# Stores to scratch on GpSimd's queue, and contraction halves of even and odd tiles, in an encoder layer

## The chip, the core and the metric

The kernel runs on one core of a Trainium2 chip. The metric is the device time of one execution in microseconds, as the median of several runs. The profile is of one execution. In it, PE is the tensor engine, ACT the scalar engine, DVE the vector engine, POOL is GpSimd, and SP is the engine that does nothing here but issue transfers. Each has a program of its own that it works through in order; an instruction that has to wait holds back all that follow it on its engine.

## What is computed

One layer of a bidirectional encoder in float32, for 1024 positions of width 2048. Cut to what matters:

```
mod = silu(c) @ w_ada + b_ada                    # 2048 x 6144
shift, scale, gate = split(mod, 3)
h = rmsnorm(x, pre_g) * (1 + scale) + shift
q, k, v, gate_a, u, gate_p = split(h @ w_in)     # 2048 x 4608
y_a = windowed_gqa(q, k, v, rel_table, sink) * silu(gate_a)
y_p = multiscale_pool(u, w_pool_grp, pool_scale) * silu(gate_p)
g_a, g_p = split(sigmoid(h @ w_merge + b_merge)) # 2048 x 4096
merged = g_a * (y_a @ w_br_attn) + g_p * (y_p @ w_br_pool)   # 1024 x 2048 each
out = x + gate * rmsnorm(merged @ w_out, post_g) # 2048 x 2048
```

## The kernel before

**Matrix products.** A float32 product is made of three float32r products: `split` writes a rounded copy `hi` on ACT and the rest `lo` on DVE, and PE forms hi·hi, lo·hi and hi·lo. On top of that the large products use Strassen's scheme in Winograd's form: `strassen` takes a weight block of 256 columns (a pair) and two halves of the contraction, and forms seven products in place of eight. The moving sides (B11, T3, T2, B21, T4, T1, B22) are made once from h and stay in SBUF; the weight sides are made anew for each pair, from the four blocks a11, a12, a21, a22 of 128 x 128 tiles that `load_raws` fetches (tag "raw", four buffers, so that a pair is fetched ahead). The products accumulate in the PSUM banks X, V and Z. A pair of four tiles a half is 84 matmuls.

**Passes.** The contraction over 2048 does not fit into SBUF at once. `PART` cuts its 16 tiles of 128 into two passes: `pass1` computes the first part for all 34 pairs of `w_in` and `w_merge` and stores it to `part_d` (four stores of 256 KB a pair, `to_dram`, L283); the second pass, `next_pair`, loads these sums (`load_parts`, L189), adds its own and stores to `proj_d`. In a pass the halves of the contraction are tiles j and j + 8. The first four pairs of the first pass run in two rounds of two tiles a half (`ramp_pair`, the ramp, with `ramp_d`), so that products can begin before all of h is there.

**The head.** Before the first pair x is loaded and normed (`fetch_rows_of_x`, `norm_rows`) and half of it turned. For each j the modulation columns of tiles j and j + 8, scale and shift, come from 16 loads of `w_ada` (`ada_slots`, L407, and `ada_tile`, L388; 4 segments of 128 columns a row) and products with c on PE (`modulation`, L421). `fill(j)` then modulates the tiles and writes the moving sides; for j = 0 and 2 GpSimd takes three subtractions (L98), for j = 1 and 3 two.

**Other work beside the pairs.** Small steps hang in a list `side` that `run` serves between products: the modulation of j = 4 to 7, the gate's row (`gate_step`, `gate_row`), the bias lines, turning the rest of x, then attention (`step`, with `ya_d`) and pooling (`window`, `mix`, with `yp_d`; two memsets of u in each window run on GpSimd). Then come the two branches (L961; `finish` multiplies by a gate from `proj_d`, stores the first branch to `mp_d` and adds it in the second, with two buffers "pv", and stores to `m_d`), the first half of the output product by Strassen (`out_pair`, `po_d`), and the rest of it with the norm and the output (`finish_rows`).

**Buffers of a pair's results.** They have the tag "ev": nine buffers at the start of the first pass, six at its end, seven in the second pass. A pair needs four for the loaded sums and three for p7, u2 and u4 (L262, `u4`, copies Z on ACT). A buffer is free once the store from it has landed.

**Order.** All transfers but seven small ones are issued by SP: `load` and `store` are both `nc.sync.dma_start`. A planner orders each engine's instructions by a model of their times, so loads and stores come mixed in SP's program.

Of the kernel before, what the change touches and what calls it, by code (L numbers as in the profile page):

```python
# [42 lines left out]
def encoder_layer(ctx: ExitStack, tc: tile.TileContext, x, c, table, w_ada, b_ada, pre_g,  # L43
# [56 lines left out]
    load = nc.sync.dma_start  # L100
    store = nc.sync.dma_start

# [8 lines left out]
    sc = const.tile([P, KT], F32, name="sc")  # L111
    modc = const.tile([P, 4, HALF], F32, name="modc")
    rstd = const.tile([P, NB], F32, name="rstd")
# [57 lines left out]

    def load_raws(w, n0, krow, js):
        raws = []
        nj = len(js)
        joint = wp.tile([P, 2, 2, nj, P], F32, tag="raw", name=uid("raw"), bufs=4) if nj < 4 else None
        for nt in range(2):
            r = joint[:, nt] if nj < 4 else wp.tile([P, 2, nj, P], F32, tag="raw", name=uid("raw"), bufs=4)
            for kh in range(2):
                r0 = krow(kh, js[0])
                load(r[:, kh], w[r0:r0 + nj * P, n0 + nt * P:n0 + (nt + 1) * P]  # L180
                     .rearrange("(k p) n -> p k n", p=P))
            raws.append(r)
        return raws

    def load_parts(ev, part):
# [5 lines left out]

    def strassen(w, n0, krow, js, op, ev, finish, part=None, raws=None):

# [6 lines left out]

        nj = len(js)
        raws = raws or load_raws(w, n0, krow, js)
        a11, a12, a21, a22 = raws[0][:, 0], raws[0][:, 1], raws[1][:, 0], raws[1][:, 1]
        parts = load_parts(ev, part) if callable(part) else part
# [104 lines left out]

    def krow1(part):  # L310
        return lambda kh, j: (kh * HALF + part * 4 + j) * P


# [25 lines left out]

    PART = [[0, 1, 2, 3, 8, 9, 10, 11], [4, 5, 6, 7, 12, 13, 14, 15]]  # L340
    xT = {}
    for s in range(2):
        for k in PART[0]:
            if k % 8 == 3:
# [12 lines left out]
    def norm_rows(si):  # L357
# [13 lines left out]
        for q in range(2):  # L371
            xt = xts[si, 2 * q]
            nc.vector.tensor_scalar(xt, xt, rstd[:, si:si + 1], None, op0=ALU.mult)
            pt = bank(("mm", SEEDED[si % 2])[q], "XT1")
            for j in range(4):
                nc.tensor.transpose(pt[:, j * P:(j + 1) * P], xt[:, j * P:(j + 1) * P], ident)
            for j in range(4):
                dst = xT[q * 8 + j, si // 4][:, (si % 4) * P:(si % 4 + 1) * P]
                if j % 2 == 0:
                    nc.vector.tensor_copy(dst, pt[:, j * P:(j + 1) * P])  # L380
                else:
                    nc.scalar.activation(dst, pt[:, j * P:(j + 1) * P], AF.Copy)

    def ada_tile(j, q):
        at = xa.tile([P, 2, 4, P], F32, tag="xa", name=uid("ada"))
        for kk in range(2):
            r0 = (2 * q + kk) * P
            load(at[:, kk], w_ada[r0:r0 + P, 0:2 * D].rearrange("p (g n) -> p g n", g=4)  # L388
                 [:, :, j * P:(j + 1) * P])
        return at  # L390
# [7 lines left out]
    def mod_columns(j, pm):  # L398
        add(modc[:, :, j], pm[:, 0:4], cols[:, 16 + j:16 + j + 25:8])
        nc.vector.scalar_tensor_tensor(modc[:, 2:4, j], modc[:, 2:4, j], 1.0,  # L400
                                       cols[:, 48 + j:48 + j + 9:8], op0=ALU.add, op1=ALU.mult)

    def ada_slots(j):
        tiles = []
        for kc in range(KT):
            tiles.append(slot("ada", F32, (P, 4, P)))
            load(tiles[kc], w_ada[kc * P:(kc + 1) * P, 0:2 * D].rearrange("p (g n) -> p g n", g=4)  # L407
                 [:, :, j * P:(j + 1) * P])
        return tiles
# [49 lines left out]
    def modulate(eng, t, k):  # L459
        kh, j = k // HALF, k % HALF  # L460
        if eng is nc.scalar:
            eng.activation(t, t, AF.Identity, scale=modc[:, 2 + kh, j:j + 1], bias=modc[:, kh, j:j + 1])
        else:
            eng.tensor_scalar(t, t, modc[:, 2 + kh, j:j + 1], modc[:, kh, j:j + 1],
                              op0=ALU.mult, op1=ALU.add)
# [13 lines left out]
    def fill(j, eng):  # L479
        (b11, b12), (b21, b22) = ((xT[k, 0], xT[k, 1]) for k in (j, j + 8))  # L480
        modulate(nc.scalar, b11, j)
        modulate(nc.vector, b12, j)
        modulate(nc.vector, b22, j + 8)
        modulate(nc.scalar, b21, j + 8)
        put(op, "B11", j, b11)
# [13 lines left out]
    claim(0)  # L499
    raws = [load_raws(*weight_of(ORDER[i]), krow1(0), [0, 1]) for i in range(RAMP)]  # L500
    ada.append(ada_slots(2))
# [25 lines left out]
    def ramp_pair(jj, i, parts, at):  # L527
        w, n0 = weight_of(ORDER[i])
        dst = block(part_d, ORDER[i]) if jj else block(ramp_d[i], 0)
        run(strassen(w, n0, krow1(0), (2 * jj, 2 * jj + 1), op, ev, to_dram(dst), parts, raws[i]),  # L530
            side, range(7), at)
# [5 lines left out]
    raws = [load_raws(*weight_of(ORDER[i]), krow1(0), (2, 3)) for i in range(RAMP)]  # L537
    fill(2, nc.gpsimd)
# [10 lines left out]
    def pass1(n, side, every):  # L549
        nonlocal i  # L550
        for k in range(n):
            w, n0 = weight_of(ORDER[i])
            run(strassen(w, n0, krow1(0), range(4), op, ev, to_dram(block(part_d, ORDER[i]))),
                side, every[k % len(every)])
# [31 lines left out]
    def gate_row(n):  # L586
# [33 lines left out]
    def fetch_x(si, q):  # L620
        xt = xin.tile([P, 512], F32, tag="xt2", name=uid("xt"))
        c0 = q * 1024 + 512
        load(xt, x[si * P:(si + 1) * P, c0:c0 + 512])
# [3 lines left out]
    def turn_x(si, q, xt):  # L627
# [3 lines left out]
        for j in range(4):  # L631
            dst = h[q * 8 + 4 + j][si // 4][:, (si % 4) * P:(si % 4 + 1) * P]
            nc.scalar.activation(dst, pt[:, j * P:(j + 1) * P], AF.Copy)
# [10 lines left out]
    side.extend(lambda k=k, s=s: modulate((nc.scalar, nc.vector)[s], h[k][s], k) for k in PART[1] for s in range(2))  # L644
    h1, h2, t2 = {j: h[4 + j] for j in range(4)}, {j: h[12 + j] for j in range(4)}, {}

# [16 lines left out]
    def next_pair(every=(0, 1, 3, 4, 6)):  # L663
        n = ORDER[pidx[0]]
        w, n0 = weight_of(n)
        run(strassen(w, n0, krow1(1), range(4), op, ev, to_dram(block(proj_d, n)),
                     block(part_d, n)), side, every)
# [232 lines left out]
    for b, w in enumerate((w_ba, w_bp)):  # L900
# [36 lines left out]
        for i in range(8):  # L937
            def finish(blk, ps, addend, res, gates=gates, i=i, b=b):
# [21 lines left out]

            run(strassen(w, i * 256, lambda kh, j: (kh * 4 + j) * P, range(4), op, ev, finish), side,  # L961
                () if b == 0 and i == 0 else (0, 2, 4) if b == 0 or i < 7 else (0, 1, 2, 3))
# [176 lines left out]
    def finish_rows(o, ssq, half, t):  # L1139
# [6 lines left out]
        for n in (1, 0, 2, 3):  # L1146
# [91 lines left out]
```

## Time and profile before

| | us |
|---|---|
| median of 3 runs | 2189.49 (2187.74 to 2189.76) |
| profiled execution, time | 2183.51 |
| profiled execution, span of its instructions | 2181.6 |
| PE busy | 2131.1 (98%) |
| DVE busy | 1480.4 (68%) |
| ACT busy | 1071.4 (49%) |
| GpSimd busy | 90.9 (4%) |
| mean granted clock of PE | 0.993 |

In a row of the timeline the columns are the start, the time that it covers, engine, line, operation, output and inputs by the program's names, shapes, count, and in brackets the idle time before it and what ended it. "SPq" is the issue of a transfer. In a table by stage each engine has its busy time and, in brackets, the number of instructions; then come the granted clock, the share of the DMA engines that was busy (a value above 1 means that transfers overlap on them) and the rate. In a table of waits the columns are the sum, the count and the longest. PE's busy time is modelled for matmuls that overlap, so it can include short stalls.

### The profile page before, as it was taken

Reading aid. Unit: us, or ns where it says so; the run is one execution under the profiler, and the core shown is the slowest. Engines: PE = TensorE matmul, PEld = TensorE weight load, DVE = VectorE, ACT = ScalarE, POOL = GpSimd, SP = SyncE. Lnnn points to the kernel's source line nnn. Section 1 sums busy time; section 2 is a strip of 40 time slices with the busy share of each in tenths; the row PEclk is TensorE's granted clock in tenths of the full one; section 3 lists DMA queues with packets and bytes.
Section 4 is the critical chain, followed back from the end, with each engine's and each line's share of the span. In section 5 each row is a group of like instructions: output and inputs, shape, how many; then the busy total and the mean of one; then the engine's idle time right before and its main releaser. Section 6 shows DMA issues by size and latency. Waiting matters only on the chain.

```text
span 2181.6 us, 30031 instructions
## 1 busy us (share of the span) xinstructions
PE 2131.1 (98%) x10253; PEld 1761.0 (81%) x10253; DVE 1480.4 (68%) x2636; ACT 1071.4 (49%) x2024; POOL 90.9 (4%) x121
## 2 busy tenths in 40 slices
PE   5999999999999999999999999999999999999998
PEld 2488888888688888888888888888787888999886
DVE  6687665666445676777776887657858878755456
ACT  5464444444366546767765433334646545323353
POOL 1100000000000000000000000000000000000363
PEclk9999999999999999999999999999999999999999
DMA  9987666664444356555545666755755654539455
GB/s 299 267 254 214 193 189 192 199 217 151 134 152 126 116 175 202 164 169 173 167 154 192 218 224 204 245 171 180 224 162 162 203 175 149 189 97 309 138 199 184
DMA packets 403180, 410.58 MB, mean 188 GB/s; under 512 B 23723, under 2 KB 279851, under 8 KB 403028
## 3 DMA queue, kind: packets, MB, share of 16 engines
q1 hardware_dynamic: 402692, 408.62, 59.3%
q8 instruction: 80, 1.31, 0.3%
q14 instruction: 72, 0.59, 0.1%
q10 hardware_dynamic: 336, 0.06, 0.0%
HBM read 295.32 MB, written 115.37 MB: 188 GB/s over the span
## 4 chain that ended last, share of the span: by engine, by line
PE 92%; DMA 3%; DVE 3%; ACT 1%; issue 1%; SPq 0%; DVEq 0%; ACTq 0%
PE Z L216 30%; PE V L216 20%; PE X L216 20%; PE OUT L1115 3%; PE OUT L1114 3%; PE OUT L1113 3%; PE OUT L1028 2%; PE OUT L1029 2%; PE OUT L1027 2%; PE GEMV L421 2%; PE PT L757 1%; DMA raw<-in_w_in_dram 1%; DMA gt<-proj_d 1%; DMA xt<-in_x_dram 1%; PE PV L768 0%
## 5 line engine op out<-in xcount | busy, mean ns | idle before, releaser
L91 ACT ACTIVATE whi<-raw 128x512 fp32r<-128x512 f32 (+1 forms) x584 | 356.1, 612 | 615.2 <-PE Z L216 274.8
L92 DVE TENSOR_TENSOR wlo<-raw,whi 128x512 fp32r<-128x512 f32 (+1 forms) x584 | 400.6, 689 | 283.1 <-PE Z L216 170.3
L1028 PE MATMUL OUT<-wlo,mh 128*128 128x256 f32 x448 | 127.5, 285 | 3.1 <-DVE wlo L92 3.0
L1027 PE MATMUL OUT<-whi,mh 128*128 128x256 f32 x448 | 126.5, 284 | 1.2 <-DVE c L941 1.2
L1029 PE MATMUL OUT<-whi,ml 128*128 128x256 f32 x448 | 126.7, 284 | 0.0
L95 DVE TENSOR_TENSOR u<-V,u 128x512 f32<-128x512 f32 x88 | 60.6, 689 | 91.2 <-PE V L216 91.0
L216 PE MATMUL V<-T3h,whi 128*128 128x512 f32 x336 | 92.6, 394 | 4.4 <-ACT whi L91 4.4
L216 PE MATMUL Z<-B22h,whi 128*128 128x512 f32 x336 | 92.4, 394 | 1.0 <-ACT u L262 1.0
L216 PE MATMUL X<-B11h,whi 128*128 128x512 f32 x336 | 92.5, 393 | 0.5 <-ACT whi L91 0.5
L216 PE MATMUL Z<-T1h,whi 128*128 128x512 f32 x336 | 92.2, 392 | 0.5 <-ACT T1h L91 0.4
L216 PE MATMUL V<-T4h,whi 128*128 128x512 f32 x336 | 92.2, 392 | 0.0
L216 PE MATMUL X<-B11l,whi 128*128 128x512 f32 x336 | 91.2, 390 | 0.0
L216 PE MATMUL Z<-T2h,whi 128*128 128x512 f32 x336 | 91.2, 391 | 0.0
L216 PE MATMUL X<-B21h,whi 128*128 128x512 f32 x336 | 90.9, 390 | 0.0
L216 PE MATMUL Z<-B22l,whi 128*128 128x512 f32 x336 | 90.9, 390 | 0.0
L216 PE MATMUL Z<-T1l,whi 128*128 128x512 f32 x336 | 90.9, 389 | 0.0
L216 PE MATMUL V<-T4l,whi 128*128 128x512 f32 x336 | 90.9, 390 | 0.0
L216 PE MATMUL V<-T3h,wlo 128*128 128x512 f32 x336 | 90.9, 390 | 0.0
L216 PE MATMUL Z<-T2h,wlo 128*128 128x512 f32 x336 | 90.8, 390 | 0.0
L216 PE MATMUL V<-T4h,wlo 128*128 128x512 f32 x336 | 90.8, 390 | 0.0
L216 PE MATMUL Z<-B22h,wlo 128*128 128x512 f32 x336 | 90.8, 389 | 0.0
L216 PE MATMUL V<-T3l,whi 128*128 128x512 f32 x336 | 90.7, 390 | 0.0
(285 smaller groups left out, 4961.3 us busy)
## 6 DMA issues: line engine op xcount, KB each, us to landing
part<-part_d SPq DMA_DIRECT2D x136, 256.0 KB
ada<-in_w_ada_dram SPq DMA_DIRECT2D x128, 256.0 KB
raw<-in_w_in_dram SPq DMA_DIRECT2D x128, 256.0 KB
raw<-in_w_merge_dram SPq DMA_DIRECT2D x128, 256.0 KB
proj_d<-part SPq DMA_DIRECT2D x68, 256.0 KB
gada<-in_w_ada_dram SPq DMA_DIRECT2D x32, 512.0 KB
gt<-proj_d SPq DMA_DIRECT2D x64, 256.0 KB
raw<-in_w_out_dram SPq DMA_DIRECT2D x32, 512.0 KB
```

The source lines that it names most:

```text
L91: nc.scalar.activation(hi, src, AF.Copy)
L92: nc.vector.tensor_tensor(lo, src, f32(hi), ALU.subtract)
L95: (eng or nc.vector).tensor_tensor(o, a, b, ALU.add)
L216: nc.tensor.matmul(ps, w_[:, i], op[mov][j][m_], start=fresh and i == 0 and n == 0, stop=i == nj - 1 and n == 2, skip_group_check=True)
L421: nc.tensor.matmul(pv[g:g + 32, :], scz[:, kc, :], tile_of(kc), start=kc < 4, stop=kc >= 12, tile_position=(0, g))
L757: nc.tensor.transpose(pt[:, i * P:(i + 1) * P], p[:, i * P:(i + 1) * P], ident)
L1027: nc.tensor.matmul(o_, hi[:, ts_], wh, start=j == 0, stop=False)
L1028: nc.tensor.matmul(o_, hi[:, ts_], wl, start=False, stop=False)
L1029: nc.tensor.matmul(o_, lo[:, ts_], wh, start=False, stop=j == KS - 1)
L1113: nc.tensor.matmul(pb, hi[:, ts_], wh, start=k == KP[0], stop=False)
L1114: nc.tensor.matmul(pb, hi[:, ts_], wl, start=False, stop=False)
L1115: nc.tensor.matmul(pb, lo[:, ts_], wh, start=False, stop=k == KT - 1)
```

## The change

It has two parts. Stores to scratch, which all go through `store`, are issued by GpSimd; loads stay on SP, and so do the stores of the output. The two small loads of `gate_row` go to GpSimd too. And the halves of the contraction in the two passes become the even and the odd tiles: part 0 is tiles 0 to 7, and tile 2j stands in one half and 2j + 1 in the other. With that the columns of `w_ada` for one j are 2 segments of 256, x is turned by its first and then its second half, and `load_raws` fetches the 256 columns of a pair in one row of 1 KB (before: two of 512 bytes in loads of their own), two loads a pair in place of four. In the branches the halves stay as they were (`rows_apart`), but the rows are of 256 columns as well. The blocks a11 to a22 become strided slices of the raw tiles.

```diff
     load = nc.sync.dma_start
-    store = nc.sync.dma_start
+    store = nc.gpsimd.dma_start
...
-    def load_raws(w, n0, krow, js):
+    def load_raws(w, n0, rows, js):
         raws = []
         nj = len(js)
-        joint = wp.tile([P, 2, 2, nj, P], F32, tag="raw", ...) if nj < 4 else None
-        for nt in range(2):
-            r = joint[:, nt] if nj < 4 else wp.tile([P, 2, nj, P], F32, tag="raw", ...)
-            for kh in range(2):
-                r0 = krow(kh, js[0])
-                load(r[:, kh], w[r0:r0 + nj * P, n0 + nt * P:n0 + (nt + 1) * P]
-                     .rearrange("(k p) n -> p k n", p=P))
+        joint = wp.tile([P, 2, nj, 256], F32, tag="raw", ...) if nj < 4 else None
+        for kh in range(2):
+            r = joint[:, kh] if nj < 4 else wp.tile([P, nj, 256], F32, tag="raw", ...)
+            load(r, rows(w, js, kh)[:, :, n0:n0 + 256])
             raws.append(r)
         return raws
+
+    def rows_apart(w, js, kh):
+        r0 = (kh * len(js) + js[0]) * P
+        return w[r0:r0 + len(js) * P].rearrange("(k p) n -> p k n", p=P)
+
+    def rows_in_turn(part):
+        def rows(w, js, kh):
+            r0 = (part * 8 + 2 * js[0]) * P
+            return w[r0:r0 + 2 * len(js) * P].rearrange("(k h p) n -> h p k n", h=2, p=P)[kh]
+        return rows
...
-        a11, a12, a21, a22 = raws[0][:, 0], raws[0][:, 1], raws[1][:, 0], raws[1][:, 1]
+        a11, a21, a12, a22 = (raws[kh][:, :, nt * P:(nt + 1) * P] for kh in range(2) for nt in range(2))
...
-    PART = [[0, 1, 2, 3, 8, 9, 10, 11], [4, 5, 6, 7, 12, 13, 14, 15]]
+    PART = [range(8), range(8, 16)]
...
-            xt = xts[si, 2 * q]
+            xt = xts[si, q]
...
-            load(tiles[kc], w_ada[kc * P:(kc + 1) * P, 0:2 * D].rearrange("p (g n) -> p g n", g=4)
-                 [:, :, j * P:(j + 1) * P])
+            load(tiles[kc].rearrange("p (g h) n -> p g (h n)", g=2),
+                 w_ada[kc * P:(kc + 1) * P, 0:2 * D].rearrange("p (g n) -> p g n", g=2)
+                 [:, :, j * 256:(j + 1) * 256])
...
     def modulate(eng, t, k):
-        kh, j = k // HALF, k % HALF
+        j, kh = k // 2, k % 2
...
-        (b11, b12), (b21, b22) = ((xT[k, 0], xT[k, 1]) for k in (j, j + 8))
+        (b11, b12), (b21, b22) = ((xT[k, 0], xT[k, 1]) for k in (2 * j, 2 * j + 1))
...
-        load(grow[:, 0, :], b_ada[0:1, 2 * D + n * 256:2 * D + (n + 1) * 256])
-        load(grow[:, 1, :], post_g[0:1, sl])
+        nc.gpsimd.dma_start(grow[:, 0, :], b_ada[0:1, 2 * D + n * 256:2 * D + (n + 1) * 256])
+        nc.gpsimd.dma_start(grow[:, 1, :], post_g[0:1, sl])
...
-            store(out[r0:r0 + P, n * 512:(n + 1) * 512], o[t][n])
+            nc.sync.dma_start(out[r0:r0 + P, n * 512:(n + 1) * 512], o[t][n])
```

The remaining lines of the diff give the new tile numbers and the new shape of `modc` to the places that use them.

More of the change, by code (lines that the diff above doesn't have):

```diff
@@ L499, in encoder_layer @@
     claim(0)
-    raws = [load_raws(*weight_of(ORDER[i]), krow1(0), [0, 1]) for i in range(RAMP)]
+    raws = [load_raws(*weight_of(ORDER[i]), rows_in_turn(0), [0, 1]) for i in range(RAMP)]
     ada.append(ada_slots(2))
@@ L529, in ramp_pair @@
         dst = block(part_d, ORDER[i]) if jj else block(ramp_d[i], 0)
[L530 removed]
+        run(strassen(w, n0, rows_in_turn(0), (2 * jj, 2 * jj + 1), op, ev, to_dram(dst), parts, raws[i]),
             side, range(7), at)
@@ L536, in encoder_layer @@
                   if i == RAMP - 1 else None)
-    raws = [load_raws(*weight_of(ORDER[i]), krow1(0), (2, 3)) for i in range(RAMP)]
+    raws = [load_raws(*weight_of(ORDER[i]), rows_in_turn(0), (2, 3)) for i in range(RAMP)]
     fill(2, nc.gpsimd)
@@ L552, in pass1 @@
             w, n0 = weight_of(ORDER[i])
-            run(strassen(w, n0, krow1(0), range(4), op, ev, to_dram(block(part_d, ORDER[i]))),
+            run(strassen(w, n0, rows_in_turn(0), range(4), op, ev, to_dram(block(part_d, ORDER[i]))),
                 side, every[k % len(every)])
@@ L665, in next_pair @@
         w, n0 = weight_of(n)
-        run(strassen(w, n0, krow1(1), range(4), op, ev, to_dram(block(proj_d, n)),
+        run(strassen(w, n0, rows_in_turn(1), range(4), op, ev, to_dram(block(proj_d, n)),
                      block(part_d, n)), side, every)
@@ L959, in finish @@
                     fetch_gate(*wanted.popleft())
-            run(strassen(w, i * 256, lambda kh, j: (kh * 4 + j) * P, range(4), op, ev, finish), side,
+            run(strassen(w, i * 256, rows_apart, range(4), op, ev, finish), side,
                 () if b == 0 and i == 0 else (0, 2, 4) if b == 0 or i < 7 else (0, 1, 2, 3))
```

45 lines of the change are left out of this document (22 added, 23 removed).

## The prediction

> **What bounds the kernel now.** I read the page first, for its totals and its chain.
>
> ```profile
> span 2181.6 us, 30031 instructions
> PE 2131.1 (98%) x10253; PEld 1761.0 (81%) x10253; DVE 1480.4 (68%) x2636; ACT 1071.4 (49%) x2024; POOL 90.9 (4%) x121
> PE 92%; DMA 3%; DVE 3%; ACT 1%; issue 1%; SPq 0%; DVEq 0%; ACTq 0%
> ```
>
> The chain that ended last lies on TensorE for 92%. Only the 3% under DMA, about 65 us, can go by better transfers, so I asked where it lies: the table by stage, then SP's and PE's timelines of the head.
>
> ```profile
> core 0: us, PE busy (x) PEld busy (x) DVE busy (x) ACT busy (x) POOL busy (x), PEclk, DMA share, GB/s
> 24.50:53.80 29.30, 23.94 (x100) 10.34 (x100) 19.09 (x62) 13.35 (x41) 4.27 (x17) 0.83 1.15 303
> 62.70:75.50 12.80, 9.76 (x21) 1.96 (x21) 10.91 (x18) 5.90 (x11) 3.32 (x2) 0.63 1.07 281
> 120.00:160.00 40.00, 40.00 (x177) 32.86 (x177) 35.70 (x74) 23.47 (x52) 2.15 (x2) 1.00 0.85 259
> 200.00:300.00 100.00, 100.00 (x451) 83.00 (x450) 64.52 (x103) 40.80 (x67) 0.00 (x0) 1.00 0.64 192
> 500.00:600.00 100.00, 96.69 (x416) 74.72 (x415) 51.12 (x79) 37.74 (x63) 0.00 (x0) 1.00 0.42 138
> 1190.00:1400.00 210.00, 210.00 (x926) 173.57 (x925) 166.77 (x282) 79.81 (x121) 0.98 (x14) 1.00 0.71 229
> 1500.00:1600.00 100.00, 99.41 (x434) 80.72 (x433) 82.54 (x132) 59.79 (x103) 0.00 (x0) 1.00 0.65 207
> 1825.00:1855.00 30.00, 26.09 (x180) 24.29 (x178) 27.63 (x45) 13.81 (x26) 0.00 (x0) 0.94 0.28 91
> ```
>
> There are two regimes. In the head the DMA engines are full (share over 1, 281 to 303 GB/s). From 200 on PE is busy throughout, at the granted clock of 1.00, with the DMA at 0.4 to 0.7: no transfer rate matters there, only single late arrivals.
>
> ```profile
> 1.22 22.97 SPq L355 DMA_DIRECT2D xt<-in_x_dram  x32
> 24.54 29.25 SPq L407 DMA_DIRECT2D ada<-in_w_ada_dram  x32
> 53.84 8.82 SPq L180 DMA_DIRECT2D raw<-in_w_in_dram  x15
> 62.76 12.66 SPq L407 DMA_DIRECT2D ada<-in_w_ada_dram  x16
> 66.50 12.01 PE L421 MATMUL GEMV<-ada,scz 128*32 128x512 f32 x26 [2.99 <-DMA ada<-in_w_ada_dram]
> 73.00 0.68 DVE L92 TENSOR_TENSOR B22l<-xT,B22h 128x512 fp32r<-128x512 f32 x1
> 78.44 0.50 PE L216 MATMUL X<-B11h,whi 128*128 128x512 f32 x1
> ```
>
> SP issues without a pause, so the queue is pushed back by the transfers. PE follows the modulation weights of j=2 as they land, 12 us for 26 records, and only at 78.44 do products of the first pair run in a row. The operands of j=1 had been ready at 73.68. The start of the steady part is thus set by how fast the weights of the first three modulations and the first raws arrive.
>
> **The change, part by part.**
>
> *Rows of 256 columns.* An x load is 256 KB in 128 rows of 2 KB: 22.97/32 = 0.718 us. A modulation load is 256 KB in 512 rows of 512 bytes: 29.25/32 = 0.914 us. The 384 rows more cost 0.196 us, 0.51 ns each. In rows of 1 KB there are 256 rows, so 0.718 + 128 x 0.00051 = 0.783 us, an estimate by this straight line: 0.131 us less. Until j=2 has landed, 32 + 16 modulation loads and the first 16 raws (128 KB each, as much as 8 loads of 256 KB) move: 56 x 0.131 = 7.3 us. The ends are nothing (if something other than the rows sets the pace) and 56 x 0.196 = 11.0 us (as fast as x). The next thing that is late is the operands of j=1: they follow the weights of j=1, so they move forward by 32 x 0.131 = 4.2, to 69.5, ahead of PE at about 71. I take -7.
>
> In the body the same edit halves SP's raw loads and the row count, with PE as the bound: 0. The four blocks of a raw tile become strided slices, four runs of 128 out of 256. The nearest strided form is a split into slices:
>
> ```profile
> L91 ACT ACTIVATE pp<-PT 128x384 fp32r<-128x384 f32 x48 | 23.2, 483 | 10.1 <-PE PT L757 9.8
> L91 ACT ACTIVATE whi<-raw 128x512 fp32r<-128x512 f32 x536 | 336.3, 630 | 586.8 <-PE Z L216 262.2 <-PE V L216 142.1 <-PE OUT L1115 63.0
> ```
>
> At 1.26 ns an element against 1.23 there is no price to be seen, and ACT and DVE idle in most pairs: 0. The first half of x in place of alternate quarters moves as many bytes, and the even and odd order is a renumbering: 0.
>
> *Stores leave SP.* In the second pass every pair issues four stores on SP in order, and the loads behind them wait:
>
> ```profile
> SPq L283 <- DVE part L95: 205.0, 56, 9.2
> SPq L283 <- ACT c L280: 189.4, 58, 7.4
> SPq L283 <- DVE u L95: 130.8, 60, 4.3
> SPq L283 <- DVE p L95: 80.6, 59, 4.7
> ```
>
> That is 606 us of SP waiting, but raws are fetched a pair ahead, so PE hardly feels it. The one clear case is at 570 to 580, from the chain in that window:
>
> ```profile
> 570.74 1.96 DMA part_d<-u
> 572.70 0.59 ACT u L262
> 574.35 0.04 SPq L283
> 574.45 3.33 DMA raw<-in_w_merge_dram
> 579.20 0.96 PE V L216 x3
> ```
>
> The raw loads of the next pair stand behind the store of p, p waits for the copy u, and u waits for the buffer that the store before frees. With the loads on a queue of their own this goes: about -3.3, PE's whole stall there; the end on the other side is 0, if the raw buffer was not free. The size is what PE idles in 500 to 600, 100 less 96.69. A gate load of the last branch came late in the same way, and PE then stood 0.97 us:
>
> ```profile
> 1668.02 0.72 ACT L930 ACTIVATE gt<-gt,cols 128x512 f32<-128x512 f32 x1 [3.12 <-DMA gt<-proj_d]
> 1673.60 1.20 PE L216 MATMUL Z<-B22h,whi 128*128 128x512 f32 x4 [0.97 <-ACT u L262]
> ```
>
> That is -1. At 1825 to 1855 PE idles 3.9 us, but DVE is busy 27.6 of 30: 0.
>
> Here the Trainium skill speaks against this part: "DMA: Bandwidth & Descriptors", section "Issuing engines are not separate DMA queues", says that issuing from several engines saves only the sequencer's issue time. By it alone this part would bring nothing and the sum would be about 2182. The rows at 570 show the other saving, a wait in program order, which the section does not count.
>
> *Stores on GpSimd.* No row shows a DMA issued there. The nearest are a store of SP, the copy u at L262 that waits for its landing, and GpSimd's own work in the ramp:
>
> ```profile
> 119.13 1.34 POOL L98 TENSOR_TENSOR xT<-tf,xT 128x512 f32<-128x512 f32 x1 [20.64 <-DVE B11l L92]
> 121.10 1.68 POOL L98 TENSOR_TENSOR xT<-xT,tf 128x512 f32<-128x512 f32 x1 [0.63 <-DVE B21l L92]
> 1420.25 0.34 SPq L283 DMA_DIRECT2D proj_d<-u  x1
> 1422.25 0.60 ACT L262 ACTIVATE u<-Z 128x512 f32<-128x512 f32 x1 [0.23 <-DMA proj_d<-u]
> 1427.49 1.07 PE L216 MATMUL Z<-B22h,whi 128*128 128x512 f32 x4
> ```
>
> SP issues a store in 0.34 us, GpSimd's operations take up to 1.7: between these lies the issue there, and with four stores in a pair (84 matmuls at 451 in 100 us, 19 us) GpSimd is busy at most 7 of 19 us. I take 1 us; it is the landing that counts. On SP the store lands 2.0 us after its issue, and already ACT waits 0.23 us for it. PE next writes that bank at 1427.49, and the copy ends at 1422.85: 4.6 us of cover. A store that lands 1 to 2 us later costs ACT that much in a pair in which it idles more, and PE nothing. Behind a store on GpSimd stand: in the ramp the subtractions of fill(2) and fill(3), in the pool stage the memsets of u. The subtractions at 119 and 121 feed T3 and T4 of the second ramp round, in a stretch where DVE is busy 35.7 of 40. A store ahead that waits for its data passes its wait on to them; I charge +2 (0 to 6, a few issues of 1.7). The row loads for the gate move to GpSimd too, ahead of the store that they already precede: 0. The output stores stay on SP, so the end has no new wait.
>
> *Sum.* -7 - 3.3 - 1 + 2 = -9.3. The profiled execution has a span of 2181.6 and a time of 2183.51, so it becomes about 2174; the median of the runs shown is 2189.49, 6 above it, and my figure goes by the median: 2180.
>
> **The rivals.**
>
> *The head gain does not come.* The pace may be set by bytes, or the list of instructions, laid out anew, puts new stalls of a few us in the body. SP's steady 0.79 us in the last 16 loads (12.66/16) speaks for it, the landing pace at PE, 26 records in 12.01 us, against. Then -3.3 - 1 + 2: about 2187, no change that can be measured.
>
> *GpSimd's stores hold VectorE (slower).* The two share a way into SBUF:
>
> ```profile
> 68.01 1.65 POOL L98 TENSOR_TENSOR xT<-tf,xT 128x512 f32<-128x512 f32 x1 [7.94 <-DVE B11l L92]
> 68.45 1.76 DVE L92 TENSOR_TENSOR T2l<-tf,T2h 128x512 fp32r<-128x512 f32 x1
> 67.84 0.69 DVE L92 TENSOR_TENSOR B21l<-xT,B21h 128x512 fp32r<-128x512 f32 x1
> ```
>
> Beside a GpSimd subtraction DVE's operation takes 1.76 us in place of 0.69. If a store's issue does the same, each costs DVE 1.07 us. In 120 to 160, 16 stores add 17 to 35.7 of 40: 13 over. In 1190 to 1400, 44 stores add 47 to 166.8 of 210: 4 over. In 1500 to 1600, 21 add 22 to 82.5: 5 over. In 1825 to 1855, about 7 add 7 to 27.6 of 30: 5 over. That is +27, less 9.3 and the ramp's +2 counted already: about 2205. It decides from some 0.2 us a store in the ramp, (40 - 35.7)/16 = 0.27. Against it: a store reads no operand through an engine. The Trainium skill, "SBUF — State Buffer", section "Who interferes with whom", says that a VectorE operation with two SBUF inputs contends only with a GpSimd instruction that reads SBUF, and that writing descriptors needs the write side; by that this rival falls, and no run here shows it.
>
> *Stores land too late (slower).* If issue and landing on GpSimd take over 2.0 + 4.6 = 6.6 us, the copy u holds PE in each of 34 pairs of the second pass. At 7.5 us that is 34 x 0.9 = 31, with the rest about 2211. For it: seven buffers in that pass and all in use. Against: the landing would have to triple.
>
> *The change does not do what it says*, in that the stores' order on GpSimd blocks as SP's did, is part of the first rival.
>
> **How the numbers follow.** The forecast has 0.56, the first rival 0.13, VectorE held 0.17, late landing 0.14. About 0.2%, 4.4 us, can be told from no change: faster below 2185, slower above 2194. The first rival is the band between; both slower rivals lie above: 0.56, 0.13, 0.31. The likeliest case alone reaches from 2189.5 - 16 = 2173 (11.0 for the rows, 5 for the stores) to 2185. For 8 in 10 the range goes on through the first rival and VectorE held, to 2208, with 2172 below; what is left out is late landing at its full price.
>
> **What would show it.** Right: the modulation rows of SP at about 0.78 us a load; PE's products of the first pair in a row from about 71 and no longer 78; no PE stall after the raw loads near 570; SP without waits at L283; DVE's two-input operations still at 0.69 us. Wrong: rows near 1.7 us on DVE beside GpSimd's stores; L262 waiting several us for a store's landing with PE waiting for it; stalls of PE between 115 and 170; a head that still ends at 78.

## The result, and the profile after

The changed kernel takes 2211.7 us (median of 6 runs, 2207.8 to 2219.7) beside 2189.6 of the kernel before on the same chip: a ratio of 1.0107, with a 95% interval of 1.0088 to 1.0126. I had forecast 2180 and a range up to 2208. It is slower, and by more than the range allowed. Its profiled execution has a time of 2214.01 us.

From the page of the profile after, the span, the busy times and the chain:

```profile
span 2211.9 us, 30103 instructions
PE 2136.0 (97%) x10253; PEld 1763.4 (80%) x10253; DVE 1482.0 (67%) x2636; ACT 1066.0 (48%) x2024; POOL 322.1 (15%) x539
PE 62%; issue 18%; DMA 9%; DVE 5%; ACT 2%; POOL 2%; SPq 0%; DVEq 0%; POOLq 0%; ACTq 0%
```

PE does the same work. Of the chain it holds 62% in place of 92; DMA, DVE and pieces without a cause have taken the rest. PE's idle time, the span less its busy time, has grown from 50.5 to 75.9 us, which is 25.4 of the 30.3 by which the span is longer. So most of the time has gone to single waits. SP's timeline of the head, and the first pair's start in PE's:

```profile
24.34 23.88 SPq L415 DMA_DIRECT2D ada<-in_w_ada_dram  x32
69.87 0.50 PE L226 MATMUL X<-B11h,whi 128*128 128x512 f32 x1
```

A load of modulation weights takes 23.88/32 = 0.746 us (before 0.914), and the first pair's products run in a row from 69.87 and no longer from 78.44. This 8.6 us lead holds through the ramp and most of the first pass, to about 545. PE's timeline shows where it is lost. In each row the first product of a pair begins; the three rows are the same three pairs in both kernels, the second 20 and the third 30 pairs behind the first. Before:

```profile
720.63 0.61 PE L216 MATMUL X<-B11h,whi 128*128 128x512 f32 x2
1190.43 0.39 PE L216 MATMUL X<-B11h,whi 128*128 128x512 f32 x1
1403.01 0.39 PE L216 MATMUL X<-B11h,whi 128*128 128x512 f32 x1
```

And after:

```profile
716.19 0.39 PE L226 MATMUL X<-B11h,whi 128*128 128x512 f32 x1
1205.49 0.39 PE L226 MATMUL X<-B11h,whi 128*128 128x512 f32 x1
1429.74 0.39 PE L226 MATMUL X<-B11h,whi 128*128 128x512 f32 x1
```

At the first of them 4.4 us of the lead are left, so some 4 were lost shortly before (under "Which stores"). Over the next 20 pairs, with attention beside them, 19.5 us are lost, and over ten more, with pooling beside them, 11.7. These 30 pairs take 1403.01 - 720.63 = 682.4 us before and 713.6 after. I use this number for the runs below and call it **the 30 pairs**. The table by stage splits it, first before, then after:

```profile
720.63:1403.01 682.38, 680.32 (x3265) 572.57 (x3264) 508.97 (x1061) 384.68 (x742) 1.12 (x16) 1.00 0.58 186
716.19:1429.74 713.55, 690.06 (x3265) 575.46 (x3264) 507.27 (x1061) 379.90 (x742) 78.21 (x159) 0.99 0.55 178
```

PE idles 2.1 us there before and 23.5 after; the other 9.7 us of the loss are longer busy time, at a granted clock of 0.99 in place of 1.00. What the engines beside PE wait for near that stretch, in the table of waits of 840 to 1400, before:

```profile
ACT sil L850 <- DMA sil<-proj_d: 11.8, 6, 3.1
DVE ws L98 <- DMA raw<-in_w_merge_dram: 5.5, 4, 2.5
DVE ws L98 <- DMA raw<-in_w_in_dram: 5.2, 4, 2.8
DVE raw L95 <- DMA raw<-in_w_in_dram: 3.0, 3, 1.4
ACT L721 <- DMA g<-proj_d: 2.9, 2, 1.5
```

And after:

```profile
ACT sil L859 <- DMA sil<-proj_d: 44.9, 7, 8.9
DVE raw L95 <- DMA raw<-in_w_merge_dram: 18.4, 6, 4.9
ACT L730 <- DMA g<-proj_d: 14.1, 7, 3.8
DVE raw L95 <- DMA raw<-in_w_in_dram: 13.4, 7, 3.9
ACT g L730 <- DMA g<-proj_d: 4.2, 1, 4.2
```

ACT and DVE stand at loads of three kinds: raw, the gate g of attention and the gate sil of pooling. In these rows the waits grow from 28 to 95 us. One of them, followed in the chain of 1250 to 1322:

```profile
1256.39 7.69 DMA sil<-proj_d
...
1265.15 0.62 ACT whi L91
...
1265.79 0.04 DVE wlo L92
...
1271.18 0.70 DVE part L95
...
1271.92 3.02 PE X L226 x12
```
```profile
1271.92 0.97 PE L226 MATMUL X<-B11h,whi 128*128 128x512 f32 x3 [2.05 <-DVE part L95]
```

The sil load lands 7.69 us after its issue. ACT, in order, had stood at it, so the next weight split on ACT is late, DVE's half of it follows, then DVE's queue up to the addition that frees the bank, and PE begins X only then, after 2.05 us without work (the row below the chain). A late load becomes PE's stall through two engines that work in order.

### The profile page after: what moved, and what is told of

Its sections match the earlier page's. It is cut to its first block, busy times and chain, and to the rows that moved or that the text cites. A ratio compares the mean times of both kernels' runs of the same rounds, so it can differ in the third digit from the quotient of the medians.

```text
span 2211.9 us, 30103 instructions
## 1 busy us (share of the span) xinstructions
PE 2136.0 (97%) x10253; PEld 1763.4 (80%) x10253; DVE 1482.0 (67%) x2636; ACT 1066.0 (48%) x2024; POOL 322.1 (15%) x539
## 4 chain that ended last, share of the span: by engine, by line
PE 62%; issue 18%; DMA 9%; DVE 5%; ACT 2%; POOL 2%; SPq 0%; DVEq 0%; POOLq 0%; ACTq 0%
PE Z L226 19%; PE V L226 13%; PE X L226 12%; PE OUT L1124 3%; PE OUT L1122 3%; PE OUT L1123 3%; PE OUT L1037 2%; PE OUT L1038 2%; PE OUT L1036 2%; DVE wlo L92 1%; DMA raw<-in_w_in_dram 1%; DMA ada<-in_w_ada_dram 1%; POOL proj_d L293 1%; DMA raw<-in_w_merge_dram 1%; PE GEMV L430 1%
## 5 line engine op out<-in xcount | busy, mean ns | idle before, releaser
L95 DVE TENSOR_TENSOR raw<-raw,raw 128x512 f32<-128x512 f32 x80 | 55.2, 690 | 85.0 <-DMA raw<-in_w_merge_dram 56.8
L293 POOL DMA_DIRECT2D proj_d<-part x68 | 36.7, 540 | 429.0 <-DVE part L95 363.8
L226 PE MATMUL Z<-T2l,whi 128*128 128x512 f32 x336 | 91.1, 390 | 0.0
L226 PE MATMUL X<-B21l,whi 128*128 128x512 f32 x336 | 90.9, 390 | 0.0
```

Source lines behind the costliest of these rows:

```text
L95: (eng or nc.vector).tensor_tensor(o, a, b, ALU.add)
L226: nc.tensor.matmul(ps, w_[:, i], op[mov][j][m_], start=fresh and i == 0 and n == 0, stop=i == nj - 1 and n == 2, skip_group_check=True)
L293: store(dst(blk), res)
```

## The experiments

Theory A: the wide raw loads in the body cause it, since the third product's a22 now comes in one load and one buffer with a12, which is freed last. Theory B: the stores on GpSimd cause it. Theory C: the instruction list, laid out anew by the planner, is worse whatever the edit is. Ratios are to the kernel before on the same chip.

### One part at a time

**e1**, the stores alone, on the kernel before (its row loads for the gate and its output stores as after):

```diff
-    store = nc.sync.dma_start
+    store = nc.gpsimd.dma_start
```

> The kernel before with the first part of the change alone: stores on GpSimd, halves and rows as before. After the whole change the head is 8.7 us earlier, and attention (840 to 1190) lost 19.7 us and pooling (1240 to 1370) 11.7 us against before. Theory A (the body's wide raw loads cause the losses, since a22, needed for the third product, shares a load and a buffer with a12, which is freed last): no loss here, the stall near 575 goes: about 2184 us. Theory B (stores on GpSimd land late, and the loads that wait for them, of ya_d, yp_d and the sums, hold DVE and ACT): the 31 us appear here without the head's gain: about 2215. Theory C (the planner's new order, whatever the edit): no rule, anywhere from 2180 to 2215.

**e2**, rows and halves alone: the kernel after with

```diff
-    store = nc.gpsimd.dma_start
+    store = nc.sync.dma_start
```

> The kernel after with its stores back on SP: even and odd halves and rows of 256 columns in head and body. Theory A: the head gains 8.7 us, attention and pooling lose about 31: about 2212 us, DVE's add of a21 and a22 waits for its raw load there as in the kernel after. Theory B: only the head's gain remains: about 2181. Theory C: anywhere from 2180 to 2215.

**e3**, as e2, but with the body's raw loads as before (`a11, a12, a21, a22 = raws[0][:, 0], raws[0][:, 1], raws[1][:, 0], raws[1][:, 1]`, four loads with rows of 512 bytes), and **e4**, the same with the stores on GpSimd:

```diff
+        if nj == 4:
+            tiles = [wp.tile([P, 2, nj, P], F32, tag="raw", ...) for nt in range(2)]
+            for nt in range(2):
+                for kh in range(2):
+                    load(tiles[nt][:, kh], rows(w, js, kh)[:, :, n0 + nt * P:n0 + (nt + 1) * P])
+            return tiles
```

> As the run with the rows alone (stores on SP), but the raw loads of the body (four tiles a half) as before: one tile for each 128 columns, four loads of 256 KB with rows of 512 bytes. Head and ramp keep rows of 256 columns. Theory A: the head's 8.7 us without the loss: about 2181 us. Theory B: 2181 as well. Theory C: anywhere from 2172 to 2205. It tells A from B only beside the run with the rows alone.

> The kernel after, stores on GpSimd, with the raw loads of the body alone as before (one tile for each 128 columns, four loads of 256 KB with rows of 512 bytes). Theory A: the head's gain and that of the stall near 575 without the loss: about 2176 us. Theory B: the loss stays: about 2212. Theory C: anywhere from 2172 to 2215.

| kernel | stores | head rows | body raws | us | ratio (95%) | the 30 pairs |
|---|---|---|---|---|---|---|
| before | SP | 512 B | 512 B | 2186.9 | 1 | 682.4 |
| e1 | GpSimd | 512 B | 512 B | 2203.6 | 1.0073 (1.0057 to 1.0090) | 697.1 |
| e3 | SP | 1 KB | 512 B | 2180.5 | 0.9973 (0.9962 to 0.9984) | 687.3 |
| e4 | GpSimd | 1 KB | 512 B | 2197.1 | 1.0050 (1.0033 to 1.0066) | 698.5 |
| e2 | SP | 1 KB | 1 KB | 2174.0 | 0.9943 (0.9931 to 0.9956) | 684.7 |
| after | GpSimd | 1 KB | 1 KB | 2211.7 | 1.0107 (1.0088 to 1.0126) | 713.6 |

This decides between A and B. The stores on GpSimd cost 16 us with the raws as before (0.73% of 2187, and e4 against e3 the same), and 36 with wide raws (1.0107 against 0.9943). The rows are a gain: 6 us by the head, 7 more by the wide raws, as long as the stores stay on SP. Theory A falls as it stood; wide raws only double the price of the stores. Of the 7 us between e2 and e3 more than half lie in the five pairs that run from 572.49 to 682.43 before. For them e3 takes 113.8 us, with a stall of PE of 3.65 at 571.76 and a granted clock of 0.77 in 570 to 585; e2 takes 109.4, without such a stall and at a clock of 1.00. In e2 the waits of the three kinds, in the same stretch:

```profile
ACT sil L859 <- DMA sil<-proj_d: 25.5, 8, 6.2
DVE raw L95 <- DMA raw<-in_w_merge_dram: 13.0, 6, 4.1
DVE raw L95 <- DMA raw<-in_w_in_dram: 7.3, 6, 2.5
ACT g L730 <- DMA g<-proj_d: 1.5, 1, 1.5
ACT L730 <- DMA g<-proj_d: 1.3, 1, 1.3
```

They are 49 us, and the 30 pairs take 684.7, 2.3 more than before: there is some room for such waits, and the kernel after has used it up.

### Which stores

On the kernel after: the stores of the passes back on SP, the rest on GpSimd (**e5**), and the reverse (**e6**; in both, the gate's two row loads stay on GpSimd); then only one of a pair's four stores back on SP (**e10**):

```diff
-            store(dst(blk), res)                                          # in to_dram
+            nc.sync.dma_start(dst(blk), res)                              # e5; e6 the reverse
+            (load if blk == "22" and ps is None else store)(dst(blk), res)  # e10
```

> The kernel after (2211.7 us) with the stores of the passes (ramp_d, part_d, proj_d) back on SP; the other stores (ya_d, yp_d, mp_d, m_d, po_d, gate and bias rows) stay on GpSimd. The rows alone, all stores on SP, had given 2174.0, so the stores cost 36 us in this layout. Theory B1 (a turn through a single buffer, g or sil, takes longer: store on GpSimd, its landing, then the next load, which stands on SP ahead of raws): the loss stays, about 2205. Theory B2 (bunching: the four stores of a pass pair no longer stand between SP's four loads of sums, so 1 MB of sums goes out at once behind or ahead of a raw or a sil load, whose landing grows from 4 to 5 us to 5 to 8): the loss goes, about 2178.

> The reverse: the stores of the passes on GpSimd as in the kernel after, all other stores on SP. Theory B1: about 2180. Theory B2: about 2205, with waits of DVE for raw loads and of ACT for sil as long as in the kernel after.

> The kernel after with one of a pair's four stores back on SP, that of p (block 22); the others stay on GpSimd. In the second pass SP's program then has that store between two loads of the sums and the other two again. In the profiles proj_d<-p lands 6.1 us after its issue on GpSimd and 3.7 on SP, and the sums 5.9 and 4.7. Theory B2 (the burst of four loads of sums, with the store of p in the middle of it on the other queue, is what makes late landings): a large part of the loss goes, 2195 to 2202, sums back near 4.7. Theory B3 (any store on the other queue costs, by its own issue and landing, since DVE and ACT have no slack in attention and pooling): a quarter of the passes' part, some 5 us: about 2205.

e5: 2195.0 us, 1.0043 (1.0028 to 1.0058), the 30 pairs 690.0. e6: 2195.6, 1.0045 (1.0030 to 1.0060), 699.7. e10: 2200.8, 1.0062 (1.0046 to 1.0079), 701.4. Each half of the stores alone costs 22 us against e2, and neither half explains the whole. By the 30 pairs the stores of the passes cost 15 us of their own (e6 against e2) and the others 5 (e5), together 29, more than the sum.

Most of e5's loss is elsewhere (7.9 us of it, against e2, from the first pair to the first of the 30), and so I found the 4 us that the kernel after loses there. The rows of the gate, stored to `pg_d` one after the other through one buffer (first and last start), in e2, after and e5:

```profile
L609 SPq DMA_DIRECT2D pg_d<-grow x8: 221/222/373, 545.6 to 611.3; - x8
```
```profile
L609 POOL DMA_DIRECT2D pg_d<-grow x8: 484/495/505, 546.3 to 638.6; - x8
```
```profile
L609 POOL DMA_DIRECT2D pg_d<-grow x8: 484/484/490, 544.2 to 690.3; - x8
```

On SP the eight rows are through at 611, in the kernel after at 639, in e5 at 690. On GpSimd a row's loads are issued in order behind the store of the row before, after its landing. In e5 SP then issues ten loads of x between 691.96 and 703.96, and PE stands 5.39 us in one piece ahead of 715.98. In the kernel after PE waits at the gate's next row and at the first turning of x:

```profile
604.01 0.60 PE L598 MATMUL b<-gacc,ones 128*1 128x256 f32 x2 [2.16 <-DVE grow L95]
647.50 0.66 PE L639 MATMUL b<-ident,xt 128*128 128x128 f32 x4 [1.29 <-ACT xt L633]
```

These are 3.45 us. The same five pairs, 572.49 to 682.43 before, (564.46 to 678.00 after) take 109.9 us before and 113.5 after: PE idles 3.3 and 4.4 us in them and is busy 2.5 us longer, at a granted clock of 0.83 in 600 to 610. How much of the 4 is the gate's doing was not tried alone; e3, with all of the gate's transfers on SP, takes 113.8 too.

### By which way

Landing times in the list of transfers of 840 to 1400, median in the last column, in the kernel after and in e5, whose stores of the passes are on SP:

```profile
part<-part_d SPq DMA_DIRECT2D x88, 256.0 KB, 5.9
proj_d<-p POOLq DMA_DIRECT2D x22, 256.0 KB, 6.1
proj_d<-part POOLq DMA_DIRECT2D x44, 256.0 KB, 2.7
```
```profile
part<-part_d SPq DMA_DIRECT2D x92, 256.0 KB, 4.6
proj_d<-p SPq DMA_DIRECT2D x23, 256.0 KB, 3.7
proj_d<-part SPq DMA_DIRECT2D x46, 256.0 KB, 2.3
```

A store from GpSimd lands 0.4 us later, the store of p 2.4, and the loads of the sums 1.3. Three ways suggested themselves: a turn through a single buffer gets longer (B1); the loads of the sums, no longer paced by the stores between them, go out at once and crowd the load that is needed (B2); each store's own delay holds up what waits for it (B3).

**B1.** Two buffers for sil (**e7**); then its load a step earlier as well, on the kernel after (**e11**) and, as a control, on e2 (**e12**):

```diff
-            sg = pp.tile([P, S], F32, tag="sil", name=f"sil{i}")
+            sg = pp.tile([P, S], F32, tag="sil", name=f"sil{i}", bufs=2)
```

> The kernel after with two buffers for sil in place of one, so that in the pooling stage a load no longer waits for the store before it to land. Theory B1: the 11.7 us of the pooling stage go, about 2200. Theory B2: the sil load goes out earlier but beside the same traffic, ACT's waits of 6 to 9 us shrink too since there is time; raws still late: 2205 to 2210.

> The kernel after with two buffers for sil and its load issued a step earlier, in the step of the window (two buffers alone had given no gain, 2209). It tests one link: that in the pooling stage ACT, standing at sil (44.9 us of waits), makes the weight splits and so DVE and PE late. If the link holds: those waits nearly vanish and the 11.7 us of pooling become 2 to 4: about 2202. If PE's losses there come from late raws instead: no gain, 2205 to 2210.

> The same edit on the kernel with the rows alone (2174.0, all stores on SP; ACT waits 25.5 us for sil there and PE loses 1.3 us in the pooling stage). If the link holds there is hardly anything to win: 2172 to 2175. It is the control for the run before.

e7: 2209.1 us, 1.0107, the 30 pairs 713.2, nothing. But four of its eight sil loads still go out some 0.06 us after a store from sil has landed, and ACT's waits for sil are still 41.4 us, so it hardly changed what it was meant to change. e11: 2204.7, 1.0082 (1.0067 to 1.0097), 705.4. Its waits for sil fell only to 36.2 us, so the link to PE was not tried as meant. The control e12: 2174.0, 0.9942, nothing. The timelines of sil say more. A turn runs from the end of the product in sil over its store and the next load to the next Silu; the median of the seven turns is 9.1 us in the kernel after and 10.2 in e2. So the turn is not longer with GpSimd's stores, and B1 falls for sil. What differs is when ACT comes to that Silu: 2.6 us after the product is ready, in place of 5.7 in e2 (medians), and from then on it stands. Whether ACT is sooner there or the product later, these rows do not show.

**B2.** The loads of the sums on GpSimd too, between the stores (**e9**); then in two groups on SP, on the kernel after (**e14**) and on e2 (**e15**):

```diff
-            load(parts[blk], part(blk))
+            nc.gpsimd.dma_start(parts[blk], part(blk))                    # e9
```
```diff
-        parts = load_parts(ev, part) if callable(part) else part
+        parts = load_parts(ev, part, ("22", "21")) if callable(part) else part   # e14, e15
...
         u2 = read("u2", "21", bz)
+        if callable(part):
+            parts.update(load_parts(ev, part, ("11", "12")))
```

> The kernel after with the loads of the sums (four of 256 KB a pair in the second pass) on GpSimd as well, so that they stand again between the stores of the pair, and SP keeps raws, kvr, qr, g, sil and u alone. Theory B1: unchanged or worse, 2205 to 2225. Theory B2: raws and sil land sooner, about 2185; if the sums themselves now come late, DVE waits for part at L95 and the gain is smaller.

> The kernel after, stores on GpSimd, with a pair's loads of the sums issued in two groups: blocks 22 and 21 at the pair's start as before, 11 and 12 only behind the third product. That brings back the pace that the stores had given SP's program, without moving a store. From pair 32 to 62 (attention and pooling) the kernel before takes 682 us, the rows alone 685, the kernel after 714. Theory B2 (bursts of four loads make the raw, sil and g loads land late): about half of the 29 us or more goes, about 2198 or below. Theory B3 (each store's own issue and landing on GpSimd, 0.5 us more, is what costs): unchanged, 2207 to 2212.

> The same edit on the kernel with the rows alone, where stores already stand between the loads. B2: hardly anything to win, 2170 to 2176. B3: the same. If it gains as much as the run before, the groups help for another reason than the pace lost with the stores.

e9: 2206.6 us, 1.0090 (1.0073 to 1.0107), 708.8. e14: 2222.2, 1.0163 (1.0148 to 1.0178), 719.0; e15: 2186.3, 0.9998, 694.5. The groups cost both layouts about 12 us: DVE now waits 25.1 us for sums, at which it had not stood in the kernel after. Waits for sil and g fell a little, those for raws did not. So the burst can be read in the landing times, but breaking it up gave nothing, and B2 is not shown to be the cause.

**B3.** Memsets on GpSimd ahead of each store to `proj_d`, first of a spare tile (**e16**), then of the result itself (**e19**, which so leaves 16 columns of each result zero and does not compute the layer; its time stands for the delay alone); and one more buffer for results, on the kernel after (**e17**) and on e13 below (**e18**):

```diff
+            if dst.second:                                   # stores to proj_d alone
+                for _ in range(5):
+                    nc.gpsimd.memset(idle_t, 0.0)            # e16
+                    nc.gpsimd.memset(res[:, 0:16], 0.0)      # e19
             store(dst(blk), res)
```
```diff
-    ev = ev_ctx.enter_context(pool("ev2", 7, side="right"))
+    ev = ev_ctx.enter_context(pool("ev2", 8, side="right"))   # e17, e18; p of attention: bufs=2
```

> The kernel after with five memsets of 16 columns on GpSimd ahead of each of the 136 stores to proj_d (about 0.1 us each, so some 0.5 us more from the result to the store's landing: as much again as GpSimd's landing, 2.7, is longer than SP's, 2.2). Theory B3: the passes' share of the loss (some 20 us) doubles, to about 2225 to 2232. Theory B2: the burst is the same, 2210 to 2216.

> The kernel after with five memsets of the first 16 columns of the result on GpSimd between a result and its store to proj_d (it leaves those columns of the projections zero). The memsets cannot be moved ahead as in the run with memsets of a spare tile. They add some 0.5 us to each of the 136 stores. If each store's own lateness costs (theory B3): 15 to 20 us more in pairs 32 to 62, about 2228. If it doesn't: 2210 to 2216.

> The kernel after with eight result buffers in the second pass in place of seven (the space comes from the buffers of p in attention, two in place of three). If a store's later landing costs by holding its buffer (SP's in-order program then stands at a load of the sums, with raws, sil and g behind it), one more buffer takes much of that: pairs 32 to 62 from 714 to 695 to 700 us, total 2193 to 2200. If the buffers are not the way, nothing or the price of the p buffers: 2208 to 2218.

> The same edit on the kernel with the rows and, on GpSimd, only the first pass's stores (2172.7, the fastest so far). By the theory of the held buffers SP's stores leave little to win: 2168 to 2173; the p buffers may cost some us. It is the control for the run before and the candidate for a faster kernel.

e16 missed its aim: the planner put the 680 memsets, which nothing ties to the stores, into the head and the ramp (1.3 to 136.3 us), where they cost some 35 us (2244.7 us, 1.0270). Its 30 pairs, otherwise those of the kernel after, take 708.6, so another layout alone can move them by 5 us. e19 did delay the stores, as GpSimd's timeline shows:

```profile
1280.42 0.79 POOL L296 MEMSET part<- 128x16 f32 x5 [8.88 <-DVE part L95]
1281.51 0.54 POOL L297 DMA_DIRECT2D proj_d<-part  x1 [0.30 <-POOL part L296]
```

Each store begins 1.09 us later than it could (the median of the 136), more than twice the 0.4 us that GpSimd's landing adds. The kernel became faster with it, 2200.0 us, 1.0073 (1.0056 to 1.0091), the 30 pairs 704.0. B3 falls: a longer delay of each store brings no loss. And these 7 us (1.0107 to 1.0073) show that e10's 10 and e11's 5 are no proof of their causes: an edit that should have cost brought as much. One more buffer (e17): 2207.6, 1.0112 (1.0086 to 1.0138), not to be told from the kernel after. Its 30 pairs take 705.7, in a profiled execution that was its fastest, 2203.3; that is no more than another layout can bring. Its control e18: 2175.1, 0.9956 (0.9939 to 0.9972), against 0.9938 of the kernel that it was built on. Held buffers are not shown to be the cause.

**What stays open.** Every kernel with a share of its scratch stores on GpSimd beyond the first pass lies at 1.0043 or above, those with wide raws and SP's stores in the later stages (e2, e12, e18 and e13 below; e15 with its groups apart) at 0.9938 to 0.9956. The loss grows with DVE's and ACT's waits for raw, sil and g. With all rows of these kinds, in 840 to 1400, the kernels line up: at 31 to 51 us of waits (before, e2, e3, e12, e13, e18) the 30 pairs take 682 to 688; at 58 (e5) 690; at 67 to 77 (e1, e4, e6, e10) 697 to 701; at 82 to 97 (e7, e9, e11, e16, e17, e19, after) 704 to 714. Only e14 and e15, with 25 us more at the sums, lie off the line (87 and 719, 44 and 694.5). That is a relation over twenty kernels and one chain that shows how; no edit removed the waits alone. What makes those loads late, the order that the planner gives SP when stores are gone from it or the traffic of two queues, was not separated. C in its strong form, no rule at all, falls; a part of each single difference, some 5 to 10 us, is C's.

### A faster kernel

e2 with the stores of the first pass, behind the ramp, on GpSimd; all others on SP:

```diff
-            run(strassen(..., to_dram(block(part_d, ORDER[i]))),
+            run(strassen(..., to_dram(block(part_d, ORDER[i]), nc.gpsimd.dma_start)),
```

> The kernel with the rows alone and, of all stores, only those of the first pass to part_d (after the ramp) on GpSimd. In the first pass up to 660 no load depends on them, and with all stores on GpSimd PE's stall near 575 (some 4.8 us) was gone and nothing else was lost before 590. All theories of the losses place them behind 590, in stages whose stores stay on SP here: 2169 to 2171. If the losses near 600 to 660 (gate row, turning of x) come from these stores too: about 2174 to 2176.

2172.7 us, 0.9938 (0.9923 to 0.9953): faster than both kernels, and not to be told from e2 at 0.9943.

## Why the prediction was wrong, point by point

- **Rows in the head, -7:** right, mis-sized by little. A load takes 0.746 us, estimated 0.783; X begins 8.6 us earlier.
- **Rows in the body, 0 "with PE as the bound":** wrong both ways. With the stores on SP they gain 7 us (e2 against e3), more than half of it near the stall that the next point is about, and with the stores on GpSimd they lose about 12 (after against e4).
- **Stall near 575, -3.3:** right in place and size: before, PE idles 3.31 us ahead of 579.20. In the chain of 566 to 582 PE now goes on without a break:

```profile
570.07 5.44 PE Z L226 x24
575.51 2.72 PE X L226 x12
578.23 2.72 PE V L226 x12
```

Either part alone does this. PE has no stall over 1.2 us there in e1, with GpSimd's stores and narrow raws, nor in e2, with SP's stores and wide raws; e3, with neither, has 3.65. So the term is not the stores' alone.

- **Row loads of the gate to GpSimd, 0:** wrong together with their store. With both on GpSimd the gate's rows end 27 us later than in e2, and the five pairs there take 3.6 us longer than before although the stall is gone; with the row loads on GpSimd and the store on SP (e6) they end at 614. I had looked at the order of these loads against their store, and not at their place in a chain through one buffer.
- **Ramp, +2:** did not come, the 8.6 us hold from the first pairs to 545.
- **The gate load of the last branch, -1:** that stretch has no gain to show; from the end of the 30 pairs, 26.7 us behind, to the pair that begins at 1807.43 before and 1837.96 after, 30.5 behind, 3.8 us more are lost.
- **Stores on GpSimd, nothing beyond the ramp:** this is the step that failed. The term was put at 0 for PE, and it is 16 us with narrow raws and 36 with wide ones. It rested on 4.6 us of cover for the copy u, read at 1420 to 1427, where neither attention nor pooling runs, and on "raws are fetched a pair ahead, so PE hardly feels it". SP's 606 us of waits at stores were taken as time that only SP loses. But raws are fetched just in time in both kernels. Before, DVE's and SP's timelines:

```profile
1420.14 0.68 DVE L92 TENSOR_TENSOR wlo<-raw,whi 128x512 fp32r<-128x512 f32 x1
1424.05 0.69 DVE L98 TENSOR_TENSOR ws<-raw,raw 128x512 f32<-128x512 f32 x1 [0.43 <-DMA raw<-in_w_merge_dram]
```
```profile
1420.85 1.00 SPq L180 DMA_DIRECT2D raw<-in_w_merge_dram  x2
```

DVE's split frees the buffer at 1420.82, the load goes out at 1420.85, and DVE stands at it from 1423.62. The row had been in the trace of before. After, SP's timeline beside DVE's:

```profile
1447.58 0.38 SPq L179 DMA_DIRECT2D raw<-in_w_merge_dram  x1
1448.06 2.58 SPq L199 DMA_DIRECT2D part<-part_d  x4
```
```profile
1453.78 0.69 DVE L95 TENSOR_TENSOR raw<-raw,raw 128x512 f32<-128x512 f32 x1 [3.43 <-DMA raw<-in_w_merge_dram]
```

The wait is 3.43 us in place of 0.43, in a stretch in which PE has no side work and does not feel it. But most of this growth is the wide raws' and not the stores'. The same wait in e1 (GpSimd's stores, narrow raws) and in e2 (SP's stores, wide raws):

```profile
1440.58 0.69 DVE L98 TENSOR_TENSOR ws<-raw,raw 128x512 f32<-128x512 f32 x1 [0.38 <-DMA raw<-in_w_merge_dram]
```
```profile
1419.76 0.69 DVE L95 TENSOR_TENSOR raw<-raw,raw 128x512 f32<-128x512 f32 x1 [2.68 <-DMA raw<-in_w_merge_dram]
```

What the stores themselves add shows in attention and pooling, where ACT and DVE also serve scores, gates and windows. In all rows of 840 to 1400 they leave the waits for narrow raws as they were (14.1 us before, 14.0 in e1) and raise those for sil from 11.8 to 33.0 and for g from 5.1 to 19.8. With wide raws all three rise from e2 to the kernel after: raws from 21.0 to 33.5, sil from 25.5 to 44.9, g from 2.8 to 18.3. The loads of sil and g, which the prediction did not look at, are thus where the stores' price appears in both layouts.
- **The rival of late landing, 2211:** it named the time, by luck: its mechanism is not there. It needed landings over 6.6 us with the copy u held. Medians are 2.7, and 6.1 for p; in the kernel after the copy (L272) waits 18.0 us over the run, all of it for PE. e19, with stores still later, is faster.
- **The rival of a held VectorE:** falls. DVE's additions with two inputs in SBUF take 690 ns (the rows `raw<-raw,raw`, 80 of them), as before, although GpSimd issues 0.54 us a store.

```profile
L95 DVE TENSOR_TENSOR raw<-raw,raw 128x512 f32<-128x512 f32 x80 | 55.2, 690 | 85.0 <-DMA raw<-in_w_merge_dram 56.8
L293 POOL DMA_DIRECT2D proj_d<-part x68 | 36.7, 540 | 429.0 <-DVE part L95 363.8
```

- **The Trainium skill's rule** ("DMA: Bandwidth & Descriptors", section "Issuing engines are not separate DMA queues") spoke against the part that failed. By it the sum would have been about 2182, and with the rows at their measured worth e2's 2174. That no more than issue time is to be won from more queues agrees with e13 against e2; that something is lost, 16 to 36 us here, it does not say.

## What to carry to other kernels

A store moved to a queue of its own changes which loads stand beside and behind which, and here its price stood where other engines, in order, wait for a load. So read the cover of a load in the busiest stage, not in a plain one, and ask of each load when its buffer comes free and when it is used: a "pair ahead" in the code can be just in time on the chip. Where two parts of a change go together, try each alone: here one was worth 12 us and hid behind the other's loss of 36.

## What had not been expected of the hardware

Rows of 1 KB in place of 512 bytes made a 256 KB load 0.168 us shorter (0.914 to 0.746), a little more than a straight line between 512 bytes and 2 KB gives (0.131). A store issued by GpSimd took 0.54 us to issue and 2.7 us to land (SP: 0.32 and 2.3). And seventeen changed kernels here with the same arithmetic (e16, with its 35 us in the head, left aside) spread from 0.9938 to 1.0163, with edits that undo a supposed cause and one that adds to it both gaining: in a program planned like this one a difference of 5 to 10 us needs more than one edit behind it.
